# Uneven conditioning steps (3, 4, 4, 5 k-tiles instead of 4, 4, 4, 4) in the first FFN of a one-core decoder block

## Chip, cores and metric

One core of one Trainium2 chip runs the kernel. The metric is the device time of one execution in microseconds. The profile is one profiled execution of the same program.

## The reference, cut to what matters

One decoder layer on 256 rows of width 2048 in float32. A conditioning vector `c` gives nine vectors of width 2048, three for each of the three sub-layers:

```python
cond = silu(c)
ada = cond @ w_ada + b_ada              # 2048 x (9*2048): shift, scale, gate for 3 sub-layers
h = rms_norm(x, g) * (1 + scale1) + shift1
x = x + 0.5 * gate1 * ((silu(h @ w_gate) * (h @ w_up)) @ w_down)   # first FFN, width 5632
...                                     # token mixing, then a second FFN of the same kind
```

The change concerns the shift and scale of the first sub-layer only, and the first FFN's gate and up products, which need `h`.

## The kernel before

**The arithmetic.** Every float32 product is made from three products of rounded parts: an activation is split in a high and a low part, and so is a weight tile. A weight unit of two k-tiles (256 rows) by 512 columns is loaded by the DMA into a `raw` buffer (512 KB), ScalarE copies it to `whi` (L136), VectorE subtracts to get `wlo` (L137), and TensorE runs 2 halves of the rows x 2 k-tiles x 3 products = 12 matmuls over 512 columns (L688 to L690 in the stretch concerned).

**The conditioning.** `ada` (L360 to L375) needs 16 row tiles of `w_ada`. Each is loaded as a `raw` tile and VectorE adds it, times a scalar of `cond`, to an accumulator `aacc` (L370 the first, L372 the other 15). For `ada_cols(0, k0, nk)` a row tile holds the shift and scale columns of `nk` k-tiles: 2 x `nk` x 128 columns, so with `nk` = 4 it is 1024 columns wide, 512 KB, in pieces of 2 KB for each of the two column ranges of a row. When all 16 are in, `by_ones` (L404) sums over the partitions with small matmuls (L407), VectorE makes `mod` (L400, L401), and `whole` and `low` (L786 to L802) make the high and low parts of `h` for those k-tiles from the transposed, scaled rows of `x` (L767 and L775).

**The steps.** `h` for all 16 k-tiles would need 32 MB of `w_ada` ahead of the first weight. So `first` (L760) and `early` (L669) work in `STEPS` (L45): the first four k-tiles' conditioning alone, then 12 column chunks (`EARLY`: gate and up of 6 chunks) over these four k-tiles while the next step's conditioning streams in between; the partial sums of each chunk are saved by ScalarE (L701) and put back into PSUM (L707) when the next step reaches the chunk. A step has 24 weight units, called w0 to w23 here, and 16 row tiles of the next step. `interleave` (L447) places the row tiles: after the u-th unit at least 16 x u / (24 - `REST`) of them are given, so with `REST` = 4 (L33) the last row tile stands between w18 and w19 and `by_ones` comes right after w19. Its ends, `then` (L821), are put on `micro`, from which one entry runs after each later unit.

**The order of work.** One list of items is walked in `run` (L139). A raw buffer (`RAW` = 6) is requested again as soon as the item that used it has been issued to VectorE, all on SP's queue (L163). The splitting of a unit and the adding of a row tile are issued at most `AHEAD` = 4 items ahead of the unit that TensorE is given, and at most `PREP` = 4 split units exist. Engines work their queues in order. Right at the start the items are 16 row tiles, then `small_cols`, `rms_first`, `scaled`, `turn` among them, and `with_raw` (L784), matmuls on row tiles 10 to 15 (`WARM`, L39) whose result nobody uses; `warm` (L778) does the same with four matmuls after `by_ones`. `load_more` (L310) puts 0.5 MB of constants into the stream during the first step.

Of the kernel before, what the change touches and what calls it, by code (L numbers as in the profile page):

```python
# [23 lines left out]
NCH = 512  # L24
# [5 lines left out]
O_KV, O_GL = 2048, 5120  # L30
O_QR, O_KR, O_VR, O_GR, O_GA, O_GB = 5168, 6192, 7216, 9264, 11312, 13360

RAW, PREP, AHEAD, T4, T2, EARLY, REST = (6, 4, 4, 6, 8, 12, 4)  # L33
SLOPES = [2.0 ** (-8.0 * (i + 1) / HEADS) for i in range(HEADS)]


LEAD = (0, 0)
BAR = 1
WARM = (10, 16, 4)  # L39
FILL = (4, 40, 320, 50, 60, 10)  # L40
SLOW = 6
HOLD = (2,2,1)
LATE = 4
GAPS = (2, 4, 3, 2)
STEPS = ((0, 4), (4, 4), (8, 4), (12, 4))  # L45
C_ID, C_D, C_BC, C_MC, C_END = 0, 128, 384, 384 + 2 * HEADS * NCMP, 384 + 2 * HEADS * NCMP + 2 * NCMP


# [20 lines left out]
def block_kernel(ctx: ExitStack, tc: tile.TileContext, I, konst, decay, out):  # L69
# [160 lines left out]
    def rows(src, kt, nk, c0, n):  # L230
        return src[kt * P:(kt + nk) * P, c0:c0 + n].rearrange("(a p) n -> p a n", p=P)
# [403 lines left out]
    def ffn(l, his, los, last, first=None, head=None):  # L635
# [33 lines left out]
        def early(ci, k0, nk, then):  # L669

            c, up = divmod(ci, 2)
            last = k0 + nk == KT

            def step(kt):
                def f(hi, lo):
                    if kt == 0 and ci == 0:
                        pairs.extend([accb(), accb()] for _ in range(2))
                    if kt == k0 and then is not None:  # L680
                        seed(then, pairs[(used[0] + 1) % 2])
                    ps = pairs[used[0] % 2]
                    for t in range(2):
                        for a in range(2):
                            xh, xl = act(kt + a, t)
                            wh, wl = by_turns(hi[:, a]), by_turns(lo[:, a])
                            kw = dict(skip_group_check=True)
                            nc.tensor.matmul(ps[t], xh, wh, start=kt + a == 0, stop=False, **kw)  # L688
                            nc.tensor.matmul(ps[t], xh, wl, start=False, stop=False, **kw)  # L689
                            nc.tensor.matmul(ps[t], xl, wh, start=False, stop=kt + a == k0 + nk - 1, **kw)  # L690
                    if kt + 2 == k0 + nk:
                        if last:
                            (up_done if up else gate_done)(c)(ps)
                            if ci == EARLY - 1:
                                pairs.clear()
                        else:
                            if k0 == 0:
                                sums[ci] = t4() if ci >= 8 else (act_hi, act_lo)[ci % 2](F32).rearrange(
                                    "p (t a) s -> p t (a s)", t=2)
                            for t in range(2):  # L700
                                nc.scalar.activation(sums[ci][:, t], ps[t], AF.Copy)  # L701
                        used[0] += 1
                return f

            def seed(i, ps):
                for t in range(2):
                    nc.scalar.activation(ps[t], sums[i][:, t], AF.Copy)  # L707
                if last or (i == 0 and k0 + nk == STEPS[-1][0]):
                    sums.pop(i)
            w = (wg, wu)[up]  # L710
            return [("w", rows(w, kt, 2, c * NCH, NCH), 2, NCH, step(kt)) for kt in range(k0, k0 + nk, 2)]

        its, sums, late, pairs, used = [], {}, [], [], [0]
        groups = ((0, 1, 2, 3), (4, 5, 6, 7), (8, 9, 10))
        if first:
            its += first(*STEPS[0])
            for i, (k0, nk) in enumerate(STEPS):
                nxt = [None if i == 0 else ci for ci in range(1, EARLY)] + [0 if i + 1 < len(STEPS) else None]
                w = [it for ci in range(EARLY) for it in early(ci, k0, nk, nxt[ci])]
                if i + 1 < len(STEPS):  # L720
                    w = interleave(w, first(*STEPS[i + 1]), len(w) - REST, *LEAD)
                its += w
# [7 lines left out]
        for gi, group in enumerate(groups):  # L730
# [3 lines left out]
            for n in range(4):  # L734
# [9 lines left out]
                k0 = group[0] * 4  # L744
# [15 lines left out]
    def first(k0, nk):  # L760
# [25 lines left out]
        def whole(k, n):  # L786

            h32 = t2([P, 2, S])
            for i in range(n):
                kt = k0 + k + i  # L790
                if kt % 4 == 0:
                    h1.append(act_hi())
                    l1.append(act_lo())
                a, b = mod[:, 1, kt:kt + 1], mod[:, 0, kt:kt + 1]
                xT = banks[(k + i) // 2][:, (k + i) % 2]
                nc.scalar.activation(h1[-1][:, kt % 4], xT, AF.Identity, scale=a, bias=b)
                nc.scalar.activation(h32[:, i], xT, AF.Identity, scale=a, bias=b)
            boxes.append((h32, (k0 + k) % 4, n, h1[-1], l1[-1]))

        def low():  # L800
            h32, k, n, hi, lo = boxes.pop(0)
            nc.vector.tensor_tensor(lo[:, k:k + n], h32[:, :n], hi[:, k:k + n].bitcast(F32), op=ALU.subtract)  # L802
# [8 lines left out]
        if k0 == 0:  # L811
            o = ada_cols(0, k0, nk, ())
            then = {0: lambda raw: small_cols(), 2: lambda raw: rms_first(), 3: lambda raw: (scaled(), turn())}
# [4 lines left out]
            for k in range(nk):  # L818
                o += [("do", lambda k=k: at_first(k)), ("prep",)]
            return o[:-1] + [("bar", BAR)]  # L820
        then = [lambda: whole(0, 2), lambda: (low(), whole(2, 2)), low] if nk == 4 else [lambda: whole(0, 2), low]  # L821
        o = ada_cols(0, k0, nk, then)
        o.insert(12, ("do", turn))
        o.insert(8, ("do", scaled))
        if k0 == STEPS[1][0]:
            o.insert(5, ("do", load_more))
# [550 lines left out]
```

## Time and profile before

| | us |
|---|---|
| median of three runs | 2462.95 (2462.95 to 2465.0) |
| the profiled execution | 2464.18 |
| its span, first to last instruction | 2462.4 |
| TensorE busy in the span | 2425.2 (98%) |
| VectorE busy | 1738.0 (71%) |
| ScalarE busy | 1219.8 (50%) |
| DMA, mean over the span | 250 GB/s |

The whole program is nearly one TensorE stream; where it is not busy is the first 37 us. The stretch that the change touches goes from the start to about 300 us. Busy shares of the whole are of little use for it, so the views below are cut to windows. Matmul durations in the trace overlap (0.38 us each at a distance of 0.216 us), so work is counted by distances between starts.

### The profile page before, as it was taken

The numbers are of one execution on the slowest core, as the hardware profiler recorded it, in microseconds if no ns is written. First come the engines' busy times: TensorE is split into PE (matmuls) and PEld (weight loads), VectorE is DVE, ScalarE is ACT, GpSimd is POOL, SyncE is SP. The second block draws the span as 40 slices with busy tenths as digits, with TensorE's granted clock in tenths as the row PEclk, the third lists the DMA queues.
The fourth block names the chain that finished last, engine by engine and source line by source line (L and its number), as shares of the span: only waits on it lengthen the run. The fifth ranks groups of instructions, "written<-read, shape, count | busy, mean of one in ns | idle before, by whom it ended". The sixth has DMA issues, their size and how long they took to land.

```text
span 2462.4 us, 31664 instructions
## 1 busy us (share of the span) xinstructions
PE 2425.2 (98%) x11616; PEld 2116.0 (86%) x11616; DVE 1738.0 (71%) x2044; ACT 1219.8 (50%) x1584; POOL 139.8 (6%) x134
## 2 busy tenths in 40 slices
PE   6999999999999999999999999999999999999999
PEld 4888888888888888888888888888888888888887
DVE  7778878989656478886667777777788554555555
ACT  4788644444445455564444444444644444444443
POOL 1000001010010111200000000000000010001001
PEclk9999999999999999999999999999999999999999
DMA  9999888899776555667887777886599666666664
GB/s 354 337 323 344 286 318 310 294 314 341 273 231 193 148 150 171 193 215 268 281 269 257 250 256 256 274 269 235 180 342 325 203 205 198 197 202 202 202 199 152
DMA packets 348264, 616.65 MB, mean 250 GB/s; under 512 B 22096, under 2 KB 79926, under 8 KB 347852
## 3 DMA queue, kind: packets, MB, share of 16 engines
q1 hardware_dynamic: 347852, 614.51, 74.5%
q8 instruction: 91, 1.49, 0.2%
q14 instruction: 65, 0.53, 0.1%
q0 software_dynamic: 256, 0.12, 0.0%
HBM read 612.45 MB, written 2.10 MB: 250 GB/s over the span
## 4 chain that ended last, share of the span: by engine, by line
PE 88%; DVE 6%; DMA 3%; issue 2%; ACT 1%; POOL 0%; SPq 0%; DVEq 0%; ACTq 0%
PE accb L240 24%; PE accb L241 24%; PE accb L239 24%; PE accb L690 3%; PE accb L688 3%; PE accb L689 3%; DVE wlo L137 2%; DVE aacc L372 2%; DMA raw<-in_w_ffn_down_dram 2%; PE mx L480 1%; DMA raw<-in_w_ada_dram 1%; PE mx L923 1%; PE mx L1160 1%; ACT whi L136 1%; PE mx L1108 0%
## 5 line engine op out<-in xcount | busy, mean ns | idle before, releaser
L137 DVE TENSOR_TENSOR wlo<-raw,whi 128x1024 fp32r<-128x1024 f32 x852 | 1048.6, 1240 | 581.9 <-ACT whi L136 576.2
L136 ACT ACTIVATE whi<-raw 128x1024 fp32r<-128x1024 f32 x852 | 893.3, 1056 | 892.8 <-PE accb L241 690.8
L239 PE MATMUL accb<-whi,ahi 128*128 128x512 f32 x3072 | 1175.3, 383 | 1.3 <-ACT ahi L537 0.9
L240 PE MATMUL accb<-wlo,ahi 128*128 128x512 f32 x3072 | 1166.1, 380 | 3.4 <-DVE wlo L137 2.5
L241 PE MATMUL accb<-whi,alo 128*128 128x512 f32 x3072 | 1165.2, 379 | 1.2 <-DVE alo L605 1.2
L240 PEld LDWEIGHTS accb<-wlo,ahi 128*128 128x128 f32 x3072 | 580.8, 189 | 88.9 <-DVE wlo L137 5.6
L241 PEld LDWEIGHTS accb<-whi,alo 128*128 128x128 f32 x3072 | 580.6, 189 | 85.7 <-DVE alo L556 1.7
L239 PEld LDWEIGHTS accb<-whi,ahi 128*128 128x128 f32 x3072 | 580.8, 189 | 82.4 <-ACT ahi L537 2.0
L372 DVE SCALAR_TENSOR_TENSOR aacc<-raw,cond,aacc 128x1024 f32<-128x1024 f32 x270 | 352.0, 1304 | 1.7 <-DMA raw<-in_w_ada_dram 0.7
L626 POOL TENSOR_TENSOR x<-x,t 128x512 f32<-128x512 f32 x50 | 80.9, 1641 | 1553.0 <-DVE t L621 1553.0
L688 PE MATMUL accb<-whi,ahi 128*128 128x512 f32 x384 | 146.6, 382 | 0.0
L690 PE MATMUL accb<-whi,alo 128*128 128x512 f32 x384 | 145.8, 380 | 0.4 <-DVE alo L802 0.4
L689 PE MATMUL accb<-wlo,ahi 128*128 128x512 f32 x384 | 146.0, 380 | 0.0
L690 PEld LDWEIGHTS accb<-whi,alo 128*128 128x128 f32 x384 | 72.7, 189 | 11.1 <-DVE alo L802 0.8
L689 PEld LDWEIGHTS accb<-wlo,ahi 128*128 128x128 f32 x384 | 72.7, 189 | 10.6 <-DVE wlo L137 0.5
L688 PEld LDWEIGHTS accb<-whi,ahi 128*128 128x128 f32 x384 | 72.9, 190 | 10.1
L605 DVE TENSOR_TENSOR alo<-mx,ahi 128x512 fp32r<-128x512 f32 x52 | 33.5, 686 | 29.4 <-ACT ahi L604 29.3
L604 ACT ACTIVATE ahi<-mx 128x512 fp32r<-128x512 f32 x52 | 28.3, 597 | 46.9 <-PE mx L480 46.9
L621 DVE TENSOR_TENSOR t<-accb,gt 128x512 f32<-128x512 f32 x56 | 36.2, 684 | 7.8 <-PE accb L241 7.8
L647 ACT ACTIVATE t<-accb 128x512 f32<-128x512 f32 x44 | 25.7, 596 | 28.6 <-PE accb L241 20.3
L1123 ACT ACTIVATE t<-t,m 128x256 f32<-128x256 f32 (+1 forms) x64 | 28.2, 443 | 18.5 <-DVE m L1114 18.5
L883 ACT ACTIVATE t<-accb 128x512 f32<-128x512 f32 x44 | 25.8, 596 | 22.8 <-PE accb L241 22.7
(196 smaller groups left out, 1049.9 us busy)
## 6 DMA issues: line engine op xcount, KB each, us to landing
raw<-in_w_ada_dram SPq DMA_DIRECT2D x288, 512.0 KB, 5.7
raw<-in_w_ffn_gate_dram SPq DMA_DIRECT2D x176, 512.0 KB, 5.1
raw<-in_w_ffn_up_dram SPq DMA_DIRECT2D x176, 512.0 KB, 4.7
raw<-in_w_ffn_down_dram SPq DMA_DIRECT2D x176, 512.0 KB, 4.2
raw<-in_w_in_dram SPq DMA_DIRECT2D x176, 512.0 KB, 4.5
raw<-in_w_in_dram SPq DMA_DIRECT2D x128, 256.0 KB, 3.9
raw<-in_w_proj_nsa_dram SPq DMA_DIRECT2D x32, 512.0 KB, 5.8
raw<-in_w_proj_ret_dram SPq DMA_DIRECT2D x32, 512.0 KB, 5.6
```

What stands on the lines that cost most here:

```text
L136: nc.scalar.activation(hi_ap, raw_ap, AF.Copy)
L137: nc.vector.tensor_tensor(lo_ap, raw_ap, hi_ap.bitcast(F32), op=ALU.subtract)
L239: nc.tensor.matmul(ps[t], xh, wh, start=kt == 0, stop=False)
L240: nc.tensor.matmul(ps[t], xh, wl, start=False, stop=False)
L241: nc.tensor.matmul(ps[t], xl, wh, start=False, stop=kt == K - 1)
L372: nc.vector.scalar_tensor_tensor(box[0], raw, k, box[0], op0=ALU.mult, op1=ALU.add)
L605: nc.vector.tensor_tensor(lo[:, 2 * b:2 * b + 2], ps, h.bitcast(F32), op=ALU.subtract)
L621: nc.vector.tensor_tensor(in_two(y), halves(ps[t]), in_two(gt[:, n * NCH:(n + 1) * NCH]), op=ALU.mult)
L626: engine.tensor_tensor(xs, xs, y, op=ALU.add)
L688: nc.tensor.matmul(ps[t], xh, wh, start=kt + a == 0, stop=False, **kw)
L689: nc.tensor.matmul(ps[t], xh, wl, start=False, stop=False, **kw)
L690: nc.tensor.matmul(ps[t], xl, wh, start=False, stop=kt + a == k0 + nk - 1, **kw)
```

## The change

The first step has 3 k-tiles, the second and third 4, the last 5. Where a step has an odd number, each chunk has a unit of one k-tile (256 KB, six matmuls) at its end. Row tiles of the first step are 768 columns wide instead of 1024 (384 KB, pieces of 1.5 KB). The conditioning of the last step, five k-tiles, is made in two parts of 3 and 2 k-tiles, with 16 row tiles each (384 and 256 KB). `REST` goes from 4 to 5, so the last row tile of a step stands between w17 and w18 and `by_ones` follows w18; in the third step, whose 32 row tiles are spread over the same 19 units, the first part ends after w9. `with_raw` runs on row tiles 9 to 12, and `warm` has three matmuls. `whole` takes k-tiles in runs of 1, 2 and the rest. The amount of matrix work is the same: 16 k-tiles x 12 chunks x 6 matmuls.

```diff
-RAW, PREP, AHEAD, T4, T2, EARLY, REST = (6, 4, 4, 6, 8, 12, 4)
+RAW, PREP, AHEAD, T4, T2, EARLY, REST = (6, 4, 4, 6, 8, 12, 5)
...
-WARM = (10, 16, 4)
+WARM = (9, 13, 3)
...
-STEPS = ((0, 4), (4, 4), (8, 4), (12, 4))
+STEPS = ((0, 3), (3, 4), (7, 4), (11, 5))
...
-            def step(kt):
+            def step(kt, n):
...
-                        for a in range(2):
+                        for a in range(n):
...
-                    if kt + 2 == k0 + nk:
+                    if kt + n == k0 + nk:
...
-            return [("w", rows(w, kt, 2, c * NCH, NCH), 2, NCH, step(kt)) for kt in range(k0, k0 + nk, 2)]
+            tiles = [(kt, min(2, k0 + nk - kt)) for kt in range(k0, k0 + nk, 2)]
+            return [("w", rows(w, kt, n, c * NCH, NCH), n, NCH, step(kt, n)) for kt, n in tiles]
...
-        then = [lambda: whole(0, 2), lambda: (low(), whole(2, 2)), low] if nk == 4 else [lambda: whole(0, 2), low]
-        o = ada_cols(0, k0, nk, then)
-        o.insert(12, ("do", turn))
+        runs = [(0, 1), (1, 2), (3, nk - 3)]
+        then = [lambda: whole(*runs[0])] + [lambda r=r: (low(), whole(*r)) for r in runs[1:]] + [low]
+        o = ada_cols(0, k0, nk, then) if nk <= 4 else ada_cols(0, k0, 3, ()) + ada_cols(0, k0 + 3, nk - 3, then)
+        o.insert(len(o) - 5, ("do", turn))
         o.insert(8, ("do", scaled))
```

## Rows read from the trace of the kernel before

**Rows 1.** The page: the span, and each engine's busy time, share of the span and instructions.

```profile
span 2462.4 us, 31664 instructions
PE 2425.2 (98%) x11616; PEld 2116.0 (86%) x11616; DVE 1738.0 (71%) x2044; ACT 1219.8 (50%) x1584; POOL 139.8 (6%) x134
```

**Rows 2.** Busy time from 30 to 40 us: the stretch, its length, the engines' busy times with instructions, the granted TensorE clock, the DMA engines' busy share and GB/s.

```profile
30.00:40.00 10.00, 9.12 (x36) 6.28 (x35) 7.11 (x10) 4.90 (x9) 0.00 (x0) 0.83 1.04 385
```

**Rows 3.** Timeline of TensorE: start, duration (us), engine, line, operation, tiles, count.

```profile
25.29 5.20 PE L784 MATMUL mx<-raw,ones 128*128 128x512 f32 x8 [3.03 <-DMA raw<-in_w_ada_dram]
...
33.56 2.10 PE L407 MATMUL mx<-ones,aacc 128*128 128x1 f32 x16 [0.29 <-DVE aacc L372]
35.52 2.05 PE L781 MATMUL mx<-ones_r 128*128 128x512 f32 x4
37.37 0.63 PE L688 MATMUL accb<-whi,ahi 128*128 128x512 f32 x1
...
43.17 0.38 PE L688 MATMUL accb<-whi,ahi 128*128 128x512 f32 x1
43.39 0.38 PE L689 MATMUL accb<-wlo,ahi 128*128 128x512 f32 x1
...
91.56 1.84 PE L407 MATMUL mx<-ones,aacc 128*128 128x1 f32 x16
93.27 0.46 PE L688 MATMUL accb<-whi,ahi 128*128 128x512 f32 x1
```

**Rows 4.** Timeline of VectorE, same columns: the rest of the first step's row tiles; then, in the first step, the last row tile of the second step and the low part of w19.

```profile
15.87 17.55 DVE L372 SCALAR_TENSOR_TENSOR aacc<-raw,cond,aacc 128x1024 f32<-128x1024 f32 x13
...
84.58 1.28 DVE L372 SCALAR_TENSOR_TENSOR aacc<-raw,cond,aacc 128x1024 f32<-128x1024 f32 x1
86.13 1.23 DVE L137 TENSOR_TENSOR wlo<-raw,whi 128x1024 fp32r<-128x1024 f32 x1 [0.28 <-ACT whi L136]
```

**Rows 5.** Busy time by stretch (columns as in group 2): the first conditioning, the restart after it, the body of the first step, and a late stretch in which most of the DMA pieces are of 1 KB.

```profile
12.00:25.00 13.00, 2.23 (x8) 1.54 (x8) 12.41 (x14) 2.36 (x6) 3.05 (x2) 1.00 1.04 386
35.00:50.00 15.00, 14.59 (x62) 12.30 (x62) 13.83 (x17) 11.08 (x17) 0.00 (x0) 0.89 0.98 336
50.00:85.00 35.00, 35.00 (x167) 30.34 (x166) 28.42 (x25) 20.91 (x27) 0.00 (x0) 1.00 1.04 385
1420.00:1430.00 10.00, 10.00 (x48) 8.77 (x47) 6.07 (x5) 4.95 (x7) 0.00 (x0) 1.00 0.92 284
```

**Rows 6.** Timeline of ScalarE: the high part of w19 in the first step, with the idle time ahead of it and what ended that.

```profile
85.05 1.06 ACT L136 ACTIVATE whi<-raw 128x1024 fp32r<-128x1024 f32 x1 [1.64 <-DMA raw<-in_w_ffn_up_dram]
```

**Rows 7.** Who waited for whom from 30 to 300 us: total, times, longest.

```profile
ACT whi L136 <- DMA raw<-in_w_ffn_gate_dram: 10.6, 13, 2.0
...
ACT whi L136 <- DMA raw<-in_w_ffn_up_dram: 8.4, 10, 1.6
...
PEld accb L689 <- DVE wlo L137: 0.5, 2, 0.3
```

**Rows 8.** Packets and the queue's share of 16 engines in two stretches: 760 to 780 us (pieces of 2 KB), then 1420 to 1430 us (mostly 1 KB).

```profile
DMA packets 1820, 3.54 MB, mean 177 GB/s; under 512 B 98, under 2 KB 98, under 8 KB 1818
q1 hardware_dynamic: 1818, 3.52, 56.2%
DMA packets 2627, 2.84 MB, mean 284 GB/s; under 512 B 153, under 2 KB 2338, under 8 KB 2626
q1 hardware_dynamic: 2626, 2.83, 91.3%
```

**Rows 9.** VectorE's groups from 103 to 168 us: line, operation, shapes, count, busy us, mean ns, idle time before and what ended it.

```profile
L137 DVE TENSOR_TENSOR wlo<-raw,whi 128x1024 fp32r<-128x1024 f32 x25 | 30.5, 1224 | 17.2 <-ACT whi L136 17.2
L372 DVE SCALAR_TENSOR_TENSOR aacc<-raw,cond,aacc 128x1024 f32<-128x1024 f32 x15 | 19.2, 1279 | 0.0
L802 DVE TENSOR_TENSOR alo<-t,ahi 128x512 fp32r<-128x512 f32 x2 | 1.4, 684 | 0.0
L370 DVE TENSOR_SCALAR aacc<-raw,cond 128x1024 f32<-128x1024 f32 x1 | 0.7, 746 | 0.0
```

**Rows 10.** Timeline of VectorE: a row tile, a low part and a row tile that follow one another without a wait.

```profile
116.98 1.28 DVE L372 SCALAR_TENSOR_TENSOR aacc<-raw,cond,aacc 128x1024 f32<-128x1024 f32 x1
118.18 1.22 DVE L137 TENSOR_TENSOR wlo<-raw,whi 128x1024 fp32r<-128x1024 f32 x1
119.31 1.28 DVE L372 SCALAR_TENSOR_TENSOR aacc<-raw,cond,aacc 128x1024 f32<-128x1024 f32 x1
```

**Rows 11.** VectorE's groups from 168 to 221 us, the third step up to its `by_ones` (columns as in group 9).

```profile
L137 DVE TENSOR_TENSOR wlo<-raw,whi 128x1024 fp32r<-128x1024 f32 x21 | 25.7, 1224 | 11.8 <-ACT whi L136 11.7
L372 DVE SCALAR_TENSOR_TENSOR aacc<-raw,cond,aacc 128x1024 f32<-128x1024 f32 x16 | 20.5, 1279 | 0.0
```

**Rows 12.** Timeline of ScalarE: the second half of a chunk's save, and the high part issued right behind it.

```profile
109.09 0.60 ACT L701 ACTIVATE ahi<-accb 128x512 f32<-128x512 f32 x1 [0.70 <-PE accb L690]
109.58 1.05 ACT L136 ACTIVATE whi<-raw 128x1024 fp32r<-128x1024 f32 x1
```

**Rows 13.** SP's queue: the eight requests (first and last) that belong to the third step and went out ahead of its first matmul, and the next pair.

```profile
150.25 0.37 SPq L163 DMA_DIRECT2D raw<-in_w_ffn_gate_dram  x1
...
163.97 0.37 SPq L163 DMA_DIRECT2D raw<-in_w_ada_dram  x1
168.20 2.17 SPq L163 DMA_DIRECT2D raw<-in_w_ffn_gate_dram  x2
```

## The prediction

> **What bounds the kernel now.** I read the page first: TensorE is busy for 2425 of 2462 us [rows 1], so the program is one matmul stream, and an edit that keeps the matmuls can only move the stream's start or put holes into it. The start comes next, in the stretches and TensorE's timeline: useful matmuls begin at 37.37 us [rows 3]. Until then VectorE adds row tiles without a pause, 13 in 17.55 us up to 33.42 [rows 4], and the DMA moves 386 GB/s with its engines fully busy [rows 5]. So the wait for the first conditioning is a wait for bytes: 8 MiB (8.39 MB) of row tiles.
>
> Then I asked whether the bytes stop binding once TensorE runs. They do not. In the body of the first step the DMA still moves 385 GB/s at full share [rows 5], and ScalarE waits for weight tiles to land, 19.0 us in 23 waits up to 300 us [rows 7]. TensorE itself waits 0.5 us for a low part [rows 7], so the supply is just in time: w19 lands at 85.05 [rows 6], its low part is ready at 87.36 [rows 4], and TensorE wants it at 89.2 (twelve matmuls of 0.216 us ahead of 91.56, plus one) [rows 3]. The step before has 1.8 us in hand there.
>
> **The change part by part.** *The start.* 2 MiB fewer: 2.10 MB at 386 GB/s is 5.4 us less. Pieces become 1.5 KB, which no row shows; by packets, 2 KB take 99 ns of an engine (56.2% of 16 x 20 us over 1818) and, with the 289 longer ones taken off, 1 KB takes 54 ns (91.3% of 160 us) [rows 8], so 1 KB costs 9% more per byte and 1.5 KB, halfway, 3%. The ends are 0 and 10% (half of the 20% that 284 GB/s at a share of 0.92 lacks against 386 at 1.04 [rows 5]; that late stretch is not all 1 KB). I take 3%: 0.5 us on 16.3. The last addition is 0.27 us shorter (1.04 ns a column, from 1224 and 684 ns for 1024 and 512 [rows 9]), and L407 loses 4 of 16 matmuls, 0.5 us of 1.96 [rows 3]. Sum: 5.4 - 0.5 + 0.3 + 0.5 = **5.7 us earlier**, matmuls from 31.7. The shorter `with_raw` and `warm` come off beside this chain; the clock is granted at 0.83 on average in 30 to 40 us as it is [rows 2], and a slower first chunk hides under the next wait.
>
> *The first step.* It has 216 matmuls instead of 288: 72 x 0.216 = 15.5 us less for TensorE. It carries the same 8 MiB of row tiles for the next step, plus 9 instead of 12 MiB of weights. Per chunk of 0.75 MiB weights and 16/19 x 2 row tiles that is 1.67 MB, 4.3 us at 386 GB/s, against 18 x 0.216 = 3.9 us of matmuls; before it was 1.89 MB in 4.9 us against 5.2. **The supply changes from just enough to too little.** The deficit grows until the last row tile is in, at w18. Up to w18 the stream then has 6 + 8 + 7.25 = 21.25 MiB where it had 8 + 8 + 10 = 26 up to w19: 4.98 MB or 12.9 us less, minus 0.5 for the pieces. So the low part of w18 is ready at 87.36 - 12.4 = 74.9; eleven more matmuls end at 77.3, `by_ones` takes 1.7 (91.56 to 93.27 [rows 3]), and the remaining 42 matmuls end the step at 88.1. Before, 48 matmuls from 93.27 end it at 103.6; less the 15.5 of moved work, 88.1. **Net 0.0 us.** Without the wait the step would end at 82.4, so 5.7 us of holes eat 5.7 us of start.
>
> Bounds: after the start, requests stall until VectorE frees buffers, and 35 to 50 us moves 336 instead of 386 GB/s, 1.9 us lost [rows 5]. If the new order loses none of it and pieces cost nothing: -2.4. If pieces cost 10% and the restart loses 1 us more, since six raw buffers then hold 2.75 instead of 3 MiB: +2.2.
>
> *Here a rule and the row part.* The stretches show 385 and 386 GB/s and no more with every engine busy [rows 5]. The Trainium skill, "DMA: Bandwidth & Descriptors", section "Bandwidth", has 425 GB/s measured for a 16 MB load and advises at least 1 MiB per DMA; at 425 the holes would be gone, while the tiles of 256 KB would be further from its advice than the old ones. No stretch of this trace's start bears 425 out; that case is the first rival.
>
> *The second step* is as before: same tiles, nothing to pay. `REST` = 5 asks 0.06 us per unit more of the DMA, covered by the five units without row tiles ahead of it.
>
> *The third step* now carries 10 MiB of row tiles in 32 pieces of work. Requests on SP go up by 16 of 0.37 us [rows 13], off the path. VectorE up to w18, by distances of 1.14 (low part) and 1.20 us (row tile) [rows 10] and 1.04 ns per column: 19 x 1.14 + 30 x 0.80 + 2 x 0.5 + lows and `mod` 2.1 = 48.8 us, of which some 3.7 (w0, w1, a row tile, lows) lie ahead of the step as before; 45.1 to do in the 51.3 us that TensorE needs (228 matmuls, the first `by_ones`, the transposes). DMA: 19.5 MiB less the eight items ordered ahead (3.4 MiB [rows 13]) is 16.9 MB, 43.8 us plus 1.3 for pieces, and 2.3 from landing to low part: also under 51.3, by over 3 us. Closest is the order: where two row tiles follow a chunk's last unit, the next but one weight is no longer within four items, so ScalarE copies it behind the chunk's save, and save end to low part ready is 0.5 + 1.05 + 1.2 us [rows 9, 12], just what TensorE takes for one unit and one matmul (2.8). That costs 0 to 0.75 us in each of the first five chunks, whose row tiles are wide, and up to 0.25 in the others: 0 to 4. I take 0.7, near the low end, since VectorE and DMA both have the time.
>
> *The fourth step*: 360 matmuls, 6.5 us a chunk; ScalarE and VectorE get 12 small tiles more, about 0.6 us each, beside TensorE. Zero, unless TensorE outruns them, then up to 0.1 us a chunk; left out. Five transposes into three PSUM banks instead of two: two pairs, three banks and `by_ones` make all eight, and nothing else asks for one there. Zero; a wait would cost one `whole`, 0.9 us.
>
> **Sum:** 0.0 + 0.7 = +0.7 us, between -2.4 and +6.2. On the profiled execution's 2464.18 that is 2464.9; the median of the runs lies 1.2 below that execution, so **2463.6**.
>
> **Rivals.** *The gain stays* (faster). If the stream could average 414 GB/s from 27.1 (last row tile of the first step in: start of its addition, less 5.0) to 67.0 (w18 landed in time for a step that ends at 82.4: 16.5 MB in 39.9 us), there would be no holes: -5.7 + 0.7, so 2458.0. By the 425 GB/s of the Trainium skill, "DMA: Bandwidth & Descriptors", section "Bandwidth", it would come so. For it in the rows: the startup loss of 1.9 us might shrink. Against it: 385 at full share over 35 us.
>
> *VectorE becomes the bound in the third step* (slower). VectorE idles 11.8 us there, all for ScalarE's high parts [rows 11]. If this idling stays, because ScalarE's copies sit behind saves that wait for TensorE, the 45.1 us become 56.9 against 51.3: 5.6 us of holes, 2468.6. It decides once more than 6.2 us of the idling remain. Against it: an engine that is behind finds its inputs ready, so idling shrinks as lateness grows.
>
> *The start does not move*, because narrower additions have a fixed part that was under-counted. The step's end hangs on bytes alone, so even 3 us less of gain leaves 2463 to 2464: the same sign as the forecast.
>
> **How the numbers follow.** A measurement here tells about 0.2% (4.9 us) from no change. Forecast 0.66 (0.02 of it slower than that bound), gain stays 0.16 (0.13 past the bound, as 2458.0 lies on its edge), VectorE 0.15, start unmoved 0.03. So faster 0.13; slower 0.15 + 0.02 = 0.17; same 0.70. The forecast alone reaches from 2460.5 to 2469.1. The range, 2459.0 to 2469.0, holds it and the VectorE case, and leaves out most of the first rival.
>
> **What would show it.** Right: first useful matmul near 31.7; holes of TensorE on low parts and landings totalling 5 to 6 us between 45 and 78; DMA at 385 there; second `by_ones` (L407) near 77 and the third about 61 us later (270 matmuls, one `by_ones`, the transposes); few holes in the third step. Wrong: no holes and `by_ones` near 71 to 72 (first rival), or VectorE without idle time and TensorE waiting for `wlo` after some 150 us (second).

## The result: 2478.0 us, slower by 0.58%

The changed kernel takes 2477.99 us (median of four runs, 2476.4 to 2478.8) against 2463.12 for the kernel before beside it: ratio 1.0058, 95% interval 1.0045 to 1.0071. That is 14.9 us slower, by the medians, and beyond the range of the prediction; the ratios here and below come from the means. The profiled executions differ by as much: the span is 2477.0 us where [rows 1] had 2462.4.

The page of the changed kernel shows little: TensorE busy 98%, as in [rows 1], 7 us more of it.

```profile
span 2477.0 us, 31789 instructions
...
PE 2432.3 (98%) x11611; PEld 2116.4 (85%) x11611; DVE 1742.8 (70%) x2076; ACT 1221.9 (49%) x1596; POOL 139.1 (6%) x134
```

TensorE's timeline shows where it went. These are its marks after the change (columns as in [rows 3]): each `by_ones` (L407), some of the holes, and the first matmul behind the four steps (L239).

```profile
28.40 1.50 PE L407 MATMUL mx<-ones,aacc 128*128 128x1 f32 x12 [1.68 <-DVE aacc L372]
29.76 0.93 PE L782 MATMUL mx<-ones_r 128*128 128x512 f32 x3
31.01 0.48 PE L688 MATMUL accb<-whi,ahi 128*128 128x512 f32 x1 [0.32 <-ACT ahi L797]
...
78.94 1.84 PE L407 MATMUL mx<-ones,aacc 128*128 128x1 f32 x16
...
140.59 1.84 PE L407 MATMUL mx<-ones,aacc 128*128 128x1 f32 x16
...
174.39 0.48 PE L689 MATMUL accb<-wlo,ahi 128*128 128x512 f32 x1 [0.78 <-DVE wlo L137]
...
186.78 1.40 PE L407 MATMUL mx<-ones,aacc 128*128 128x1 f32 x12
...
216.41 0.95 PE L407 MATMUL mx<-ones,aacc 128*128 128x1 f32 x8
...
232.34 0.48 PE L688 MATMUL accb<-whi,ahi 128*128 128x512 f32 x1 [1.92 <-ACT accb L707]
...
308.80 0.48 PE L689 MATMUL accb<-wlo,ahi 128*128 128x512 f32 x1 [0.86 <-DVE wlo L137]
...
317.32 0.38 PE L239 MATMUL accb<-whi,ahi 128*128 128x512 f32 x1
```

I went through every matmul between these marks and added up the distances above 0.216 us: a hole where TensorE waited, slow clock where matmuls follow at about 0.43 us, the pace of the lower level, 1.2 GHz. The same for the kernel before:

| stretch (from one `by_ones` to the next) | before, us lost | after, us lost | predicted change | measured change |
|---|---|---|---|---|
| start: first useful matmul at | 37.37 | 31.01 | -5.7 | -6.4 |
| first step: holes + slow clock | 0.97 + 0.59 | 6.46 + 3.12 | +5.7 | +8.0 |
| second step, up to 140.59 after | 0.16 | 0.88 | 0 | +0.7 |
| third step, all holes: up to 186.78 + up to 216.41 after | 0.17 | 5.64 + 4.07 | +0.7 | **+9.5** |
| third step without its losses | 64.65 long | 66.11 long | 0 | +1.5 |
| fourth step: holes + slow clock | 0.42 | 3.93 + 1.48 | 0 | **+5.0** |
| sum; L239 stands at | 299.02 | 317.32 | +0.7 | +18.3 |
| from there to the end | 2163.4 | 2159.7 | 0 | -3.7 |

The 1.5 us that the third step takes without any loss are the second `by_ones` of the last conditioning, which now runs in the middle of the stream (the row at 186.78). Of the last line, 1.9 us lie in the 261 us behind the mark (TensorE busy 258.0 us there before and 259.9 after); where the other 1.8 are I did not find.

Who waited for whom from 30 to 300 us, the view of [rows 7]: the wait of ScalarE for weights to land grew from 19.0 to 35.1 us (adding two rows), and TensorE's for low parts from 0.5 to 12.5 (weight loads).

```profile
ACT whi L136 <- DMA raw<-in_w_ffn_gate_dram: 18.7, 19, 1.7
ACT whi L136 <- DMA raw<-in_w_ffn_up_dram: 16.4, 17, 3.4
PEld accb L689 <- DVE wlo L137: 12.5, 15, 1.1
```

The stretches (columns as in [rows 2]) show the DMA after the change: the first step, the third step as a whole, then its first and its second part.

```profile
50.00:75.00 25.00, 22.48 (x97) 18.36 (x96) 19.96 (x20) 15.05 (x23) 0.00 (x0) 0.93 1.02 369
155.00:210.00 55.00, 50.80 (x233) 41.06 (x232) 44.82 (x49) 37.37 (x55) 0.00 (x0) 1.00 0.96 321
160.00:186.00 26.00, 22.58 (x97) 17.40 (x96) 21.15 (x21) 18.01 (x27) 0.00 (x0) 1.00 1.01 346
186.00:207.00 21.00, 20.22 (x96) 16.55 (x95) 16.30 (x21) 14.39 (x21) 0.00 (x0) 1.00 0.92 298
```

The first and third stretch are to be set beside the third of [rows 5]: 385 GB/s at a share of 1.04. Now TensorE has holes, ScalarE waits for landings, and yet the DMA brings 369 and 346 GB/s, with a share that still reads as full. **The supply is short while the DMA moves less than the rate that the prediction took to be its limit.** That was to be explained.

### The profile page after: what moved, and what is told of

The parts are those of the page before. It is cut to its first block, busy times and chain, and to the rows that moved or that the text cites. A ratio compares the mean times of both kernels' runs of the same rounds, so it can differ in the third digit from the quotient of the medians.

```text
span 2477.0 us, 31789 instructions
## 1 busy us (share of the span) xinstructions
PE 2432.3 (98%) x11611; PEld 2116.4 (85%) x11611; DVE 1742.8 (70%) x2076; ACT 1221.9 (49%) x1596; POOL 139.1 (6%) x134
## 4 chain that ended last, share of the span: by engine, by line
PE 86%; DVE 5%; DMA 4%; ACT 2%; issue 2%; POOL 0%; SPq 0%; DVEq 0%; ACTq 0%
PE accb L240 25%; PE accb L239 25%; PE accb L241 25%; PE accb L689 2%; PE accb L688 2%; PE accb L690 2%; DVE wlo L137 2%; DMA raw<-in_w_ffn_up_dram 1%; PE mx L480 1%; DMA raw<-in_w_ada_dram 1%; ACT whi L136 1%; DVE aacc L372 1%; DMA raw<-in_w_ffn_gate_dram 1%; PE mx L925 1%; PE mx L1162 1%
## 5 line engine op out<-in xcount | busy, mean ns | idle before, releaser
L137 DVE TENSOR_TENSOR wlo<-raw,whi 128x1024 fp32r<-128x1024 f32 (+1 forms) x864 | 1048.7, 1223 | 589.3 <-ACT whi L136 581.6
L136 ACT ACTIVATE whi<-raw 128x1024 fp32r<-128x1024 f32 (+1 forms) x864 | 896.8, 1044 | 929.4 <-PE accb L241 700.5
L239 PE MATMUL accb<-whi,ahi 128*128 128x512 f32 x3072 | 1175.3, 383 | 1.3 <-ACT ahi L537 1.0
L241 PE MATMUL accb<-whi,alo 128*128 128x512 f32 x3072 | 1165.2, 379 | 0.8 <-DVE alo L605 0.8
L241 PEld LDWEIGHTS accb<-whi,alo 128*128 128x128 f32 x3072 | 580.6, 189 | 85.4 <-DVE alo L556 1.7
L239 PEld LDWEIGHTS accb<-whi,ahi 128*128 128x128 f32 x3072 | 580.7, 189 | 82.3 <-ACT ahi L537 2.0
L372 DVE SCALAR_TENSOR_TENSOR aacc<-raw,cond,aacc 128x1024 f32<-128x1024 f32 (+2 forms) x285 | 355.4, 1247 | 1.0
L605 DVE TENSOR_TENSOR alo<-mx,ahi 128x512 fp32r<-128x512 f32 x52 | 33.5, 686 | 28.1 <-ACT ahi L604 28.1
```

The source lines that it names most:

```text
L136: nc.scalar.activation(hi_ap, raw_ap, AF.Copy)
L137: nc.vector.tensor_tensor(lo_ap, raw_ap, hi_ap.bitcast(F32), op=ALU.subtract)
L239: nc.tensor.matmul(ps[t], xh, wh, start=kt == 0, stop=False)
L241: nc.tensor.matmul(ps[t], xl, wh, start=False, stop=kt == K - 1)
L372: nc.vector.scalar_tensor_tensor(box[0], raw, k, box[0], op0=ALU.mult, op1=ALU.add)
L605: nc.vector.tensor_tensor(lo[:, 2 * b:2 * b + 2], ps, h.bitcast(F32), op=ALU.subtract)
```

## The experiments

The theory that the runs led to: the six raw buffers count items, not bytes. Before, six items were 6 x 512 KB = 3 MiB. Now a third of the first step's weight bytes come in units of 256 KB, and the third step's row tiles 384 and 256 KB; the mean item, by the mix per unit, is 443 KB in the first step (2.6 MiB in six buffers), 431 and 351 KB in the two parts of the third (2.5 and 2.1 MiB). By the theory the DMA delivers less when less is requested ahead. "Third step" below is the time from `by_ones` at 140.59 to that at 216.41, 75.8 us in the changed kernel, 66.1 without its holes. Rivals: VectorE's 32 row tiles; the shorter pieces; ScalarE's order of work; `load_more`; the edits beside the steps (`REST`, `WARM`, runs of activations). Marks come from one profile of each kernel. In five profiles with the same first step the second `by_ones` stands at 78.9 to 81.1, and in three with the same third step that takes 74.3 to 75.8 us, so a difference of 1 to 2 us between single profiles says little there.

**The side edits alone** (changed kernel, even steps):

```diff
-STEPS = ((0, 3), (3, 4), (7, 4), (11, 5))
+STEPS = ((0, 4), (4, 4), (8, 4), (12, 4))
```

> The changed kernel with its steps set back to 4, 4, 4, 4 k-tiles; the other edits stay (last row tile one unit earlier, shorter warm-up, runs of 1, 2, 1). If the uneven steps cost the 14.9 us, it is within 2 us of the kernel before (2461 to 2465). If the side edits cost a good part of it, 2468 or more.

Measured: 2466.88 us, ratio 1.0013 [1.0004, 1.0023]: 3.3 us slower by the means (3.8 by the medians), and L239 at 301.32. So most of the loss belongs to the uneven steps, not all.

**VectorE's row tiles.** One kernel leaves out most columns of the later additions of the last conditioning and loads every byte. The other leaves out nearly all of the bytes and keeps the width of the additions, by adding columns of `x`, which is there anyway:

```diff
-                    nc.vector.scalar_tensor_tensor(box[0], raw, k, box[0], op0=ALU.mult, op1=ALU.add)
+                    b, r = (box[0][:, :16], raw[:, :16]) if few else (box[0], raw)
+                    nc.vector.scalar_tensor_tensor(b, r, k, b, op0=ALU.mult, op1=ALU.add)
```

> The changed kernel; in the five-k-tile conditioning each of the 30 later additions covers 16 columns instead of 768 or 512, so VectorE does some 22 us less in the third step while every byte is still loaded (five k-tiles of the first sub-layer's h come out wrong). Theory supply (bytes land late in the third step): holes stay, 2475 to 2479. Theory VectorE (additions delay the low parts): the third step's holes of some 10 us and the 4 us behind them go, 2463 to 2467.

```diff
+                elif few:
+                    b = box[0]
+                    nc.vector.scalar_tensor_tensor(b[:, :16], raw, k, b[:, :16], op0=ALU.mult, op1=ALU.add)
+                    nc.vector.scalar_tensor_tensor(b[:, 16:], x[:, 0, 16:2 * width], k, b[:, 16:], op0=ALU.mult, op1=ALU.add)
...
-        its = [("a", src(w_ada[kt * P:(kt + 1) * P, :]), 2, width, step(kt)) for kt in range(KT)]
+        its = [("a", src(w_ada[kt * P:(kt + 1) * P, :]), 2, 8 if few else width, step(kt)) for kt in range(KT)]
```

> The changed kernel; the 32 row tiles of the five-k-tile conditioning load 16 columns instead of 768 or 512, and VectorE adds columns of x of the full width in their place, so its work and the order stay and 10 MiB of loads go (five k-tiles of h come out wrong). Theory supply: holes of the third step go, and the wait at the fourth step's start with them, 2463 to 2467. Theory VectorE: 2475 to 2479.

With the additions shortened: 2477.5 us, 1.0058 [1.0043, 1.0073], as the changed kernel; third step 75.4 us against 75.8. VectorE is not what holds it. With the bytes gone: 2474.05, 1.0041 [1.0027, 1.0055], third step 70.0, between the two forecasts. This run is less clear than it was meant to be: in place of each row tile VectorE does two operations, and it is busy for 25.6 of 26 us from 160 to 186 us, so here VectorE may be what is left.

**Piece length.** The last conditioning's row tiles taken as one long piece per row (from other columns of `w_ada`, so other values):

```diff
+            if lay == 0 and k0 >= STEPS[-1][0]:
+                return w[:, 2 * k0 * P:2 * (k0 + nk) * P].rearrange("p (i c) -> p i c", i=2)
```

> The changed kernel; the 32 row tiles of the five-k-tile conditioning have the same bytes, but each partition's columns lie in one piece (3 and 2 KB) instead of two of 1.5 and 1 KB (other columns of the weights, so five k-tiles of h come out wrong). If short pieces make the supply slow, half or more of the third step's holes go: 2466 to 2473. If it is the bytes or the VectorE work, within 2 us of the changed kernel: 2476 to 2480.

2477.78 us, 1.0058 [1.0043, 1.0073]; third step 74.5 instead of 75.8, which is within the spread of the profiles. The pieces are not the loss.

**Order, `load_more`, and an earlier start of the third step's row tiles.**

```diff
-RAW, PREP, AHEAD, T4, T2, EARLY, REST = (6, 4, 4, 6, 8, 12, 5)
+RAW, PREP, AHEAD, T4, T2, EARLY, REST = (6, 4, 6, 6, 8, 12, 5)
```

> The changed kernel with splits and additions issued up to 6 items ahead of TensorE's unit instead of 4. Theory order (with two row tiles behind a unit, four items reach one weight unit only, so ScalarE copies the next behind the chunk's save): it explains what was left of the third step's holes with tiny loads, some 4 us; they go: 2473 to 2475. Theory supply alone: 2476 to 2479.

```diff
-        if k0 == STEPS[1][0]:
-            o.insert(5, ("do", load_more))
...
+    items.append(("do", load_more))
```

> The changed kernel with the 0.5 MB of constants loaded at the start of the first down projection instead of in the first step. Theory supply in the first step: 0.52 MB at 370 to 385 GB/s is 1.4 us that TensorE does not wait for; by_ones of the first step some 1.4 us earlier and 2475.5 to 2477.5. If the first step is not bound by bytes: no change, 2477 to 2479.

```diff
+            fills = [first(*s) for s in STEPS[1:]]
+            pre, fills[2] = fills[2][:8], fills[2][8:]
...
+                if i == 1:
+                    at = [j for j, it in enumerate(w) if it[0] == "w"][-5:-1]
+                    for j in reversed(at):
+                        w[j + 1:j + 1] = [pre.pop(), pre.pop()][::-1]
```

> The changed kernel; the first 8 of the last step's 32 row tiles stand behind w19 to w22 of the second step (two each), where the DMA has time, and the other 24 are spread over the third step. Theory supply (too many bytes ahead of their due time in the third step): third step from by_ones to by_ones 4 us or more shorter than 75.8, the wait at the fourth step's start shorter too: 2470 to 2474. Theory order alone: at most 1.5 us shorter, 2476 to 2479.

The order: 2485.34, 1.0088 [1.0073, 1.0103]; slower than either forecast; the third step takes 75.2 us, no real change, and behind L239 the profile is 5.0 us longer. `load_more` put off: 2477.13, 1.0055 [1.004, 1.007], not told from the changed kernel; the second `by_ones`, expected 1.4 us earlier, stands at 79.78. Eight row tiles moved to where the DMA has time (the five units without row tiles ahead of the third step; 198 GB/s from 142 to 160 us): 2474.95, 1.0043 [1.0026, 1.006], third step 72.4. That is 3.4 us back where the supply theory asked for 4 or more: more than the order alone was given, less than forecast, and so no more than a hint at the supply.

**The number of raw buffers**, the test of the theory. A seventh (512 KB) takes the room of two small work buffers, so that change alone is run too, and both in the kernel before:

```diff
-RAW, PREP, AHEAD, T4, T2, EARLY, REST = (6, 4, 4, 6, 8, 12, 5)
+RAW, PREP, AHEAD, T4, T2, EARLY, REST = (7, 4, 4, 6, 6, 12, 5)
```

> The changed kernel with 7 raw buffers instead of 6, paid for with two fewer of the 2 KB work buffers (6 instead of 8; this alone can cost time later, so it is read up to 320 us in the trace). If smaller tiles leave too few bytes in flight for six buffers (the DMA went 346 to 370 GB/s at full busy share where the old tiles had 385), the rate in the first and third step rises to 380 and over and their holes shrink by a third or more. If the rate is the DMA's own for such tiles, nothing changes there.

```diff
-RAW, PREP, AHEAD, T4, T2, EARLY, REST = (6, 4, 4, 6, 8, 12, 5)
+RAW, PREP, AHEAD, T4, T2, EARLY, REST = (6, 4, 4, 6, 6, 12, 5)
```

> The changed kernel with 6 raw buffers and the smaller work pool (6 instead of 8) alone. It is the other half of the seven-buffer run: up to 315 us nothing changes (first matmul of the unbroken chunks at 315 to 318), later it costs what that run gave back, 0 to 4 us: 2477 to 2482.

The kernel before with seven and six, then with five raw buffers:

```diff
-RAW, PREP, AHEAD, T4, T2, EARLY, REST = (6, 4, 4, 6, 8, 12, 4)
+RAW, PREP, AHEAD, T4, T2, EARLY, REST = (7, 4, 4, 6, 6, 12, 4)
```

> The kernel before (steps 4, 4, 4, 4) with 7 raw buffers and the smaller work pool. Theory buffers: six of 512 KB are enough there (385 GB/s), so its first by_ones in the stream stays at 91.6 within 0.8 us and only the work pool's price shows: 2463 to 2467. If a seventh buffer helps any kernel: by_ones earlier and 2461 or less.

```diff
-RAW, PREP, AHEAD, T4, T2, EARLY, REST = (6, 4, 4, 6, 8, 12, 4)
+RAW, PREP, AHEAD, T4, T2, EARLY, REST = (5, 4, 4, 6, 8, 12, 4)
```

> The kernel before with 5 raw buffers instead of 6: 2.5 MiB in flight, about what six of the changed kernel's mixed tiles hold. Theory buffers: the first step's DMA rate from 50 to 85 us falls from 385 to 340 to 370 GB/s and TensorE gets holes there, by_ones 93 to 98 instead of 91.6, 2466 to 2478. If the rate hangs on the size of the tiles itself: 380 and over, by_ones within 0.8 us, 2462 to 2466.

| kernel | us | ratio to before | second `by_ones` | L239 |
|---|---|---|---|---|
| changed | 2477.99 | 1.0058 [1.0045, 1.0071] | 78.94 | 317.32 |
| changed, 7 raw, 6 small | 2469.80 | 1.0029 [1.0019, 1.0039] | 76.23 | 306.28 |
| changed, 6 raw, 6 small | 2482.67 | 1.0078 [1.0063, 1.0093] | 79.51 | 314.91 |
| before, 7 raw, 6 small | 2463.82 | 1.0003 [0.9993, 1.0012] | 91.47 | 298.92 |
| before, 5 raw | 2488.53 | 1.0102 [1.0085, 1.0119] | 94.41 | 303.94 |

The stretches of three of them: the changed kernel with seven, then the kernel before with seven, then with five.

```profile
60.00:75.00 15.00, 14.17 (x69) 12.06 (x69) 13.38 (x14) 9.54 (x16) 0.00 (x0) 1.00 1.04 386
160.00:186.00 26.00, 24.49 (x115) 20.04 (x114) 23.87 (x27) 19.64 (x29) 0.00 (x0) 1.00 1.05 368
```

```profile
50.00:85.00 35.00, 35.00 (x168) 30.75 (x167) 28.86 (x25) 22.14 (x28) 0.00 (x0) 1.00 1.05 385
```

```profile
50.00:85.00 35.00, 33.32 (x154) 27.43 (x153) 26.75 (x22) 19.60 (x28) 0.00 (x0) 1.00 1.00 351
```

In the kernel before tiles and order stay as they were, and with five buffers (2.5 MiB) it falls from 385 to 351 GB/s and gets holes (4.1 us in the first step). The changed kernel with seven (3.0 MiB in the first step) is back at 386, with the same 256 KB units, and 11.0 us come back up to L239, 8.2 in the total. (Against the run with six small work buffers and six raw ones, which differs by the raw buffer alone, it is 8.6 and 12.9.) Its third step rises to 368 only, not to the 380 that was asked for. The five-buffer kernel's total missed its forecast of 2466 to 2478, since 18 of its 25 us lie behind L239. With seven the kernel before gains nothing, as it already had enough requested. So in the first step the lost rate is a matter of the room in the raw buffers, and that is shown from both sides. This room is an upper limit of what is requested ahead: a buffer stays taken after its landing, until ScalarE and VectorE have read it. An estimate from the times of issue and landing in the traces gives what was on the way on average, over 50 to 85 us (50 to 75 with uneven steps): 2.05 MiB in the kernel before, 1.75 in the changed one, 2.10 with seven buffers and 1.66 in the kernel before with five. Taken by slices of 1 us from nine such profiles, the mean rate is 347 GB/s with some 1.5 MiB on the way, 372 with 2.0 and 380 with 2.5, with much scatter. And room alone does not set the rate. While only row tiles stream, the kernel before with five buffers moves 387 GB/s, with an estimated 1.85 MiB on the way from 15 to 25 us:

```profile
12.00:25.00 13.00, 2.23 (x8) 1.53 (x8) 12.38 (x14) 2.36 (x6) 3.02 (x2) 1.00 1.05 387
```

The two small work buffers have their own price, 4.7 us in the changed kernel by the medians; 2.3 of it stand late in the program, where TensorE now waits at L1162.

**Everything that helped, together** (the edits for early row tiles and a later `load_more`, and these):

```diff
-RAW, PREP, AHEAD, T4, T2, EARLY, REST = (6, 4, 4, 6, 8, 12, 5)
+RAW, PREP, AHEAD, T4, T2, EARLY, REST = (7, 4, 4, 6, 6, 12, 5)
...
-WARM = (9, 13, 3)
+WARM = (9, 16, 4)
```

> The changed kernel with all that eased its supply: 7 raw buffers (smaller work pool), 8 row tiles of the last step already behind the second, constants loaded later, and the dummy matmuls of the start kept up to the last row tile (9 to 15, then 4). Theory buffers: first by_ones in the stream at 73 to 76, third step by_ones to by_ones 69 or less, 2463 to 2467, about the kernel before. If something else holds it: 2469 or more.

2470.35, 1.0029 [1.0018, 1.0039]. Not better than seven buffers alone, and outside what the theory asked for (2463 to 2467, a third step of 69 or less): the second `by_ones` comes at 74.91, but the third step takes 71.2 us. That the earlier row tiles cure the same short supply as the seventh buffer would explain it, and was not tried alone.

**What holds the third step with a mended supply?** It takes 69.9 us with seven buffers, 3.8 of them holes. Four runs on top of seven buffers: additions shortened as above; `AHEAD` 6; row tiles placed by columns instead of by number (the wide ones come first, so placing by number asks most in the first half); and eight buffers, paid for with `PREP` 3.

> Changed kernel with seven raw and six work buffers, and the 30 later additions of the five-k-tile conditioning cover 16 of their 768 or 512 columns (left out: the rest of that sum; loads, waits and their number unchanged). Seven buffers alone had 69.9 us from the second by_ones to that of the third step's second part, against 66.3 us of matrix work. If VectorE's row tiles hold the third step back once the supply is mended (0.6 to 0.75 us less for each of 30): 67.0 us or less, total 2466.5 to 2468. If it is the order of ScalarE's copies behind saves, or the DMA: 69.3 to 70.5 us, total 2469 to 2470.5.

```diff
-RAW, PREP, AHEAD, T4, T2, EARLY, REST = (6, 4, 4, 6, 8, 12, 5)
+RAW, PREP, AHEAD, T4, T2, EARLY, REST = (7, 4, 6, 6, 6, 12, 5)
```

> Changed kernel with seven raw and six work buffers and AHEAD 6 instead of 4 (splitting and adding issued up to six items ahead). If the third step's remaining holes come from high parts that stand behind a chunk's save in ScalarE's order: 68.0 us or less between the by_ones (69.9 with AHEAD 4). If they come from the supply or VectorE: 69.3 us or more. Later stages lose by AHEAD 6 (some 7 us in the changed kernel), so the total should stay above 2472 either way; the step's own length decides.

```diff
-        nf = sum(f[0] == "a" for f in fill)
+        size = lambda f: f[3] if f[0] == "a" else 0
+        nf = sum(map(size, fill))
...
-                    given += fill[k][0] == "a"
+                    given += size(fill[k])
```

> Changed kernel with seven raw and six work buffers, and the 32 row tiles of the last step placed by columns instead of by number (wide ones 1.4 per unit, narrow ones 2.1, so that the first part ends after w11 instead of w9). With placing by number the first ten units ask 0.63 MB of row tiles and 0.52 of weights each, 1.15 MB per 2.6 us or 445 GB/s, the others 0.94 MB or 364. If this unevenness makes the holes that are left in the third step (69.9 us between the by_ones, 3.8 of them holes, with 368 GB/s at full share in its first half): 67.0 to 68.3 us, total 2467.5 to 2469. If it is the sum of the bytes: 69.5 to 70.5, total 2469.5 to 2470.5.

```diff
-RAW, PREP, AHEAD, T4, T2, EARLY, REST = (6, 4, 4, 6, 8, 12, 5)
+RAW, PREP, AHEAD, T4, T2, EARLY, REST = (8, 3, 4, 6, 8, 12, 5)
```

> Changed kernel with eight raw buffers, the room taken from the split units (PREP 3 instead of 4); small work buffers as they were. If the holes that seven buffers left in the third step (3.8 of 69.9 us) come from too few bytes in flight for tiles of 256 and 384 KB: DMA 375 GB/s or more from 160 to 186 us, 68.5 us or less between the by_ones, and, since the work buffers are kept, a total of 2463 to 2468. If the sum of the bytes or the smaller pieces make them: 343 to 370 GB/s as with seven, 69 us or more. One split unit less may cost holes of its own all over the kernel (over 2470 then), which only the first 300 us tell apart.

| on top of seven buffers | us | third step, us | DMA 160 to 186 us |
|---|---|---|---|
| nothing | 2469.80 | 69.9 | 368 GB/s, share 1.05 |
| shortened additions | 2470.89 | 70.4 | 369, 1.05 |
| `AHEAD` 6 | 2471.57 | 69.2 | 367, 1.04 |
| placed by columns | 2472.02 | 71.3 | 343, 1.00 |
| eight buffers, `PREP` 3 | 2507.26 | 70.9 | 368, 1.04 |

My expectation that the uneven placing makes the holes failed outright. VectorE, relieved of 10 of its 24 busy us in that stretch, makes no difference; the order's 0.7 us are within the spread of the profiles. With eight buffers (3.4 MiB in the first part) the DMA stays at 368, where the first step reaches 387. So more in flight does not help there, and 368 GB/s is what this mix of 2, 1.5 and 1 KB pieces got in four of these five runs. Whether it is the pieces or the sum of the bytes that then makes the 3 to 4 us of holes was not separated, and stays open. (One split unit fewer costs 37 us, 33.5 of them behind L239 by the profiles; over the program ScalarE waits 888 us for L241 to free split units, against 792 with seven buffers and `PREP` 4.)

**Which side edit costs 2 to 3 us?** Even steps with the old `WARM`, and the kernel before with `REST` 5 and nothing else:

```diff
-WARM = (9, 13, 3)
+WARM = (10, 16, 4)
```

> Even steps (4, 4, 4, 4), WARM (10, 16, 4) as before, and of the side edits only REST 5 and activations in runs of 1, 2, 1. The same with WARM (9, 13, 3) took 2466.88, 3.3 us over the kernel before run beside it, with 2.1 us of slow clock in the first step against 0.6. If the shorter warm-up made that: slow clock 0.6 us again, total 2464.5 to 2465.5. If REST or the runs made it: 2466.4 to 2467.3.

```diff
-RAW, PREP, AHEAD, T4, T2, EARLY, REST = (6, 4, 4, 6, 8, 12, 4)
+RAW, PREP, AHEAD, T4, T2, EARLY, REST = (6, 4, 4, 6, 8, 12, 5)
```

> The kernel before with REST 5 instead of 4 and nothing else. Even steps with all side edits but the shorter warm-up left the fourth step about 2 us later than before, counting the one unit (2.6 us) by which by_ones moves ahead of the matmuls, with 3.8 us of holes in the first step. If the earlier end of the row tiles does that: by_ones at 90.5 to 91, 3 to 4 us of holes and slow clock in the first step, first chunk with all k-tiles 2 to 3 us later than 299.0, total 2465 to 2466.5. If the three runs of activations do it: first step's holes near 1.5, total 2463 to 2464.

The old warm-up: 2466.32, 1.0009 [1.0000, 1.0019]. My expectation for it was wrong in an instructive way. The clock is granted in full, as these stretches show (first the short warm-up, then the old one), yet the second `by_ones` comes at 90.92 instead of 90.75.

```profile
36.00:40.00 4.00, 4.00 (x11) 2.95 (x11) 3.26 (x7) 3.27 (x7) 0.00 (x0) 0.50 1.02 350
```

```profile
36.00:40.00 4.00, 3.84 (x14) 2.28 (x13) 3.53 (x7) 3.69 (x8) 0.00 (x0) 1.00 1.04 383
```

Slow clock in that step falls from 2.10 to 0.21 us and the holes grow from 1.14 to 3.77: with the bytes as the limit, a faster TensorE just waits longer. `REST` 5 alone: 2465.13, 1.0008 [0.9999, 1.0017], not told from no change by the runs; in its profile the first step loses 3.45 us instead of 1.56 and L239 stands 2.1 us later, at 301.09, close to the 301.3 and 301.5 of the two kernels with all side edits. So by these profiles the side edits' cost up to L239 is `REST`: it asks for the last row tile one unit (2.6 us) sooner, and the step before had 1.8 us in hand at most.

## Why the prediction was wrong, step by step

**The start** was right: `by_ones` 5.2 us earlier, as its sum had it, and the first useful matmul at 31.01 against 31.7 (in the kernel before four warm-up matmuls stood right ahead of it without a pause, now three, while the sum had set them beside the chain). The DMA moved 372 GB/s from 10 to 20 us with pieces of 1.5 KB, 3.6% under the 386 of [rows 5]; I had taken 3%.

**The first step**: right mechanism, rate too high. The gain of the start was eaten by waits for bytes, as said, and with seven buffers the second `by_ones` stands at 76.2 (I had 77.3). With six it stood at 78.94 (at 79.4 to 81.1 in four other profiles with the same first step, and at 83.7 in the one without the last row tiles' bytes; why they differ I can't explain), and the DMA ran slower: from 28.4 to 74.9 us it moved 364 GB/s, and 381 with seven buffers. The 17.7 MB that 381 brings in that time need 48.7 us at 364, 2.2 more; the marks lie 2.7 apart. The other profiles fit: the later the `by_ones`, the lower the rate (362, 358, 353, 352, then 348 GB/s). My upper bound named the very thing, "six raw buffers then hold 2.75 instead of 3 MiB", but priced it as 1 us, once, after the start. In the runs the rate was lower for the whole of the step.

**The third step failed**, in the sentence "DMA: 19.5 MiB less the eight items ordered ahead (3.4 MiB [rows 13]) is 16.9 MB, 43.8 us plus 1.3 for pieces ... under 51.3, by over 3 us". It took 385 GB/s for items of 256 to 512 KB. Between 155 and 210 us the DMA moved 321 GB/s: 17.7 MB in 55 us, which at 385 would be 45.9. The 9.1 us between these are near the 9.5 us of holes by which the step grew. Seven buffers give 5.9 of them back (75.8 to 69.9; 4.4 against the profile with six small work buffers), so that much is the room; what makes the other 3.6, at 368 GB/s, stays open. The sum also left out the second `by_ones` in the stream, 1.5 us. The row to look at stood in the trace of before all along: with 512 KB items, six buffers gave 385 and nothing to spare [rows 5, 7], and no row showed that rate with smaller ones; that was a cost without a row, to be bounded, and I carried the rate over instead.

**VectorE, my slower rival**, is refuted for its mechanism, though one of its signs showed: TensorE did wait for low parts. VectorE was not without idle time. From 150 to 217 us, a longer stretch than the 53 us of [rows 11], it idles 14.2 us for high parts, about as much per us as before.

```profile
L137 DVE TENSOR_TENSOR wlo<-raw,whi 128x1024 fp32r<-128x1024 f32 x20 | 24.5, 1225 | 14.4 <-ACT whi L136 14.2
```

But one link further on, ScalarE did not stand behind its saves: of those 14.2 us much is its own wait for landings, as the waits from 142 to 217 us show, and shortened additions changed nothing.

```profile
ACT whi L136 <- DMA raw<-in_w_ffn_gate_dram: 8.8, 7, 1.7
...
ACT whi L136 <- DMA raw<-in_w_ffn_up_dram: 5.1, 4, 3.4
```

**The first rival**, the gain that stays, did not come. The most in any 10 us of any run is some 403 GB/s (400 from 1790 to 1800 us in the kernel before with seven buffers), and some 391 in the first 200 us. The Trainium skill, "DMA: Bandwidth & Descriptors", section "Bandwidth", gives 425 GB/s for one 16 MB load, measured on loads that GpSimd issued. These runs, whose loads go out from SP, do not reach it. The same section advises at least 1 MiB per DMA. By that rule the 256 KB units would be the fault. But the changed kernel with seven buffers moves 386 GB/s with the same units, so in the first step it is the sum of what is requested that counts, and not one transfer's size.

**The fourth step**, costed at nothing, lost 5.0 us. ScalarE has ten activations for the five k-tiles, and a late conditioning put them right ahead of a chunk's seed. ScalarE's timeline shows it busy without a pause up to the seed (L707) for which TensorE waited 2.1 us:

```profile
226.99 1.09 ACT L701 ACTIVATE t<-accb 128x512 f32<-128x512 f32 x2
227.94 0.60 ACT L797 ACTIVATE ahi<-mx,mod 128x256 fp32r<-128x256 f32 x1
228.39 0.60 ACT L798 ACTIVATE t<-mx,mod 128x256 f32<-128x256 f32 x1
228.84 0.61 ACT L797 ACTIVATE ahi<-mx,mod 128x256 fp32r<-128x256 f32 x1
229.29 0.61 ACT L798 ACTIVATE t<-mx,mod 128x256 f32<-128x256 f32 x1
229.74 2.06 ACT L136 ACTIVATE whi<-raw 128x1024 fp32r<-128x1024 f32 x2
231.63 1.18 ACT L707 ACTIVATE accb<-ahi 128x512 f32<-128x512 f32 x2
```

The clock is granted at 0.79 on average from 230 to 238 us, hole and what follows, which adds 1.5 us. With seven buffers the hole is 1.3 us and no slow clock follows. That the late third step is what makes it worse is my reading of these two; it was not tried alone.

**The account.** Of 14.9 us, at least 8.2 are the room of the raw buffers (seven give that back, though the small buffers they replace cost 4.7). What is left with seven stands, by its profile, up to L239: -5.7 for the start, +4.6 in the first step, +0.7 in the second, +3.6 of holes and +1.5 for the second `by_ones` in the third, +2.5 in the fourth, 7.3 in all by the marks (306.28 against 299.02); behind it the profile is 2.1 shorter than that of before, with L1162's 2.3 in it. About 2 of the first step's 4.6 may be `REST`, by the profile of that edit in the kernel before. No version with uneven steps beat the kernel before; the best is 2469.8.

## What to carry to other kernels

A ring of buffers is sized in items, while what kept the DMA at its rate here was bytes on the way: whoever makes tiles smaller in a stretch that lives on the full rate should add buffers, or count a lower rate for the whole stretch. How much room is enough depends on how long a buffer stays taken after its landing: 2.5 MiB did at the start of the program and did not beside the splitting of weights. A DMA share of 1.0 does not prove that the DMA can do no more; hold GB/s against the best stretch. And where bytes set the pace, moving the deadline of a load by one unit (`REST`) can cost time too: 2.1 us at L239 in a profile, though the runs alone do not tell it from nothing.

## What the runs showed that I had not expected

- The DMA's rate in the first step (50 to 75 us, 50 to 85 with even steps; 2 KB pieces mostly) against what the raw buffers hold: 381 to 386 GB/s at 3.0 MiB or more, 341 to 369 at 2.6 in six profiles, 351 at 2.5 in one; the share reads 1.04 to 1.05, 0.98 to 1.02 and 1.00. The share gives away only half of the loss.
- At the start, with row tiles alone, pieces of 1.5 KB ran at 372 GB/s with six buffers and at 374 with seven (12 to 25 us), so there the room was not the limit.
- Short holes in a long stream can be followed by the lower clock: from 62 to 66 us, behind two holes of 1.1 and 1.0 us, the granted clock is 0.60; holes of 0.7, 0.5 and 1.0 us between 169 and 175 us had no such effect (1.00 from 160 to 186). Nor had holes of 0.9 and 1.0 us at 212.7 and 213.9 (1.00 from 214 to 218), nor, with seven buffers, holes of 1.15 and 1.04 us at 59.7 and 60.9 (1.00 from 60 to 75). What decides it, these runs do not show.

```profile
62.00:66.00 4.00, 3.75 (x10) 3.07 (x11) 3.27 (x5) 1.84 (x3) 0.00 (x0) 0.60 1.02 369
...
230.00:238.00 8.00, 6.08 (x20) 4.71 (x20) 7.11 (x8) 7.34 (x11) 0.00 (x0) 0.79 0.61 203
```
